# A 32-byte tile first on the left side of SBUF

## The chip, the cores and the metric

The kernel runs on one core of a Trainium2 chip. The metric is the device time of one execution in microseconds (us). The engines are PE (TensorE, matrix products), PEld (its weight loads), DVE (VectorE), ACT (ScalarE), POOL (GpSimd) and SP (SyncE, which issues the DMAs).

## The reference

Two transformer blocks of two layers each run one after the other on a stream of 512 tokens x 1024 channels, all in float32. The first block's layer is

```
h = rms_norm(x, g_mix[l])
q_a, k_a, v_a, u_b, cq, ckv, kpe, gate_logits = split(h @ w_in[l])
y_a, y_b, y_c = swa_attention(...), conformer_conv(...), mla_attention(...)
branches = einsum('bsnc,ncd->bsnd', stack([y_a, y_b, y_c], axis=2), w_branch[l])
x = x + einsum('bsnd,bsnd->bsd', sigmoid(gate_logits), branches) @ w_out[l]
h = rms_norm(x, g_mlp[l])
x = x + square(relu(h @ w_up[l])) @ w_down[l]
```

The second block adds a context of 256 tokens and scales and shifts each norm by a condition (six vectors from `silu(c) @ mod_w + mod_b`). Its first layer mixes with a differential attention and an rwkv7 recurrence, its second with a state space scan and a gated linear attention. Both end as above: `x = x + g1 * (o @ w_out)`, then `x = x + g2 * (square(relu(h @ w1)) @ w2)`, hidden width 4096. Most of the arithmetic is in products of a weight matrix with all tokens.

## The kernel before

Everything is feature-major: a stream is eight tiles of 128 channels x 512 tokens (256 for the context). A weight matrix is read in tiles of 128 rows x up to 1024 values, eight blocks of 128 x 128.

A float32 product is made of three faster ones. `split` (line 196) writes an operand as `hi` + `lo`, both of type fp32r, and `load_w` (line 209) does that to a weight tile: a DMA brings `raw`, ACT casts it to `whi`, DVE writes the rest as `wlo`. `mm3` (line 225) then adds three products into one PSUM tile:

```
t.matmul(ps, w[0], x[0], start=start, stop=False)    # line 228: whi, hi
t.matmul(ps, w[0], x[1], start=False, stop=False)    # line 229: whi, lo
t.matmul(ps, w[1], x[0], start=False, stop=stop)     # line 230: wlo, hi
```

The first operand is the stationary one, the weights (128 x 128); the second is the moving one (128 x 512 or 128 x 256). Each of the three loads its weights anew. `gemm` (line 232) does this for the eight (or four) blocks of an output tile; a group of 24 products of 512 columns in a row is the common case. `gemm_group` and `gemm_level` do it for several output tiles at once.

The order of the work is that of the code: generators are advanced alternately by `weave` (line 176), and each engine takes its instructions as they were written. Waits between engines are added by the framework.

**Where tiles lie.** SBUF is filled from both ends. A pool opened with `side="right"` takes its place downward from the far end, the others upward from the near one, and tiles get addresses rounded to 32 bytes. The first pool on the left is `const` (line 52), with `ident` first; after 16 KiB of scratch and four constants, `ident` stands at byte 16512 of each partition. The streams `x` (`streams`, line 129) and most pools of weights are on the right. The split operands (tags h, hc, u2 and others) are mostly on the left, in the first layer of the second block's mixers and in the last layer's features also on the right. Tiles of a kind all have sizes that are multiples of 512 bytes, so each kind has one place modulo 512.

The table counts the program's fp32r products by the columns of the moving operand and by the start addresses of moving operand and weights modulo 512; d is weights minus moving, modulo 128. The letter is used later.

| group | columns | moving | weights | d | products | where (an example in us) |
|---|---|---|---|---|---|---|
| A (main) | 512 | 192 | 480 | 32 | 7,548 | first block, last MLP (3655 to 3990) |
| B | 512 | 384 | 480 | 96 | 1,536 | `mlp2` of the first layer (3177) |
| C | 256 | 384 | 480 | 96 | 1,744 | the same, context (2665) |
| D | 512 / 256 | 480 | 480 | 0 | 808 / 728 | mixers' inputs, `odd_late` (3400) |
| E | 512 | 416 | 480 | 64 | 416 | mixers' inputs of the first layer |
| F | 256 | 192 | 480 | 32 | 384 | start of the last MLP (3632) |
| G | 512 / 256 | 288 | 288 | 0 | 136 / 168 | `out_proj` (256 columns: 2596) |
| H | 512 / 256 | 288 | 480 | 64 | 120 / 120 | `out_proj`, later tiles (2602 to 2646) |
| I | 512 | 224 | 224 | 0 | 96 | `out_proj`, first tiles (2587) |

Besides, some 4,100 products are in full float32 (small ones in the attentions and recurrences); each is run as two passes, transposes as one.

Of the kernel before, what the change touches and what calls it, by code (L numbers as in the profile page):

```python
# [20 lines left out]
P = 128  # L21
# [6 lines left out]
class Build:  # L28
# [6 lines left out]
    # ---------------------------------------------------------------- helpers  # L35
# [14 lines left out]
    def setup(self):  # L50
        nc = self.nc
        self.const = self.pool("const")
        self.wp = self.xp = None
        self.sp = None
        self.cvs, self.md = {}, []
        self.ident = self.const.tile([P, P], F32, name="ident")
        self.ones = self.const.tile([P, P], F32, name="ones")
        nc.vector.memset(self.ones, 1.0)
        self.mhalf = self.const.tile([P, 32], F32, name="mhalf")
        nc.gpsimd.memset(self.mhalf, -0.5)  # L60

    def consts(self, which, later=False):
        """load a block of packed constants into the innermost phase; later: returns a function that loads it."""
        t = self.tl([P, CV_COLS[which]], F32, "cv")
        self.cvs[which] = t
        load = lambda: self.nc.sync.dma_start(out=t, in_=self.A[which])
        return load if later else load()
# [17 lines left out]
    def phase(self, side=None, **bufs):  # L85
        """chunks with these tags (tag=buffers) while the returned context is open."""
# [18 lines left out]
    def scope(self, attr, **kw):  # L105
        """self.<attr> is a fresh pool while the returned context is open."""
# [17 lines left out]
    def weights(self, parts=2, **kw):  # L124
        """a pool for the weights; parts: tiles of each split part"""
        self.wparts = parts
        return self.scope("wp", **kw)

    def streams(self):
        """a pool for the residual streams, at the far end of the memory"""  # L130
# [26 lines left out]
    def banks(self, **bufs):  # L157
        """PSUM tags (tag=buffers) while the returned context is open."""
# [17 lines left out]
    def weave(main, back=(), until=None):  # L176
        """Alternates the steps of generators: main is [(gen, steps)], kept level until all of them (or the one
        named) end; back is [(task, rate)], tasks that advance rate steps with every main step and may go on later."""
# [16 lines left out]
    # x*scale(+bias) split exactly into two fp32r parts  # L195
# [29 lines left out]
    def mm3(self, ps, w, x, start, stop):  # L225
        """ps (+)= w.T @ x for operands split as (hi, lo)."""
# [5 lines left out]
    def gemm(self, src, xs, n=T, m=P, w=None, tag="g"):  # L232
        """one output tile [m, n] of W.T @ x; src is DRAM [128, kc*m]."""
# [8 lines left out]
    def gemm_group(self, srcs, xs, n=T, ws=None, pieces=1):  # L242
        """several output tiles level in the contraction, for operands that arrive one after another (in pieces of
        their columns); returns their PSUM tiles and weights."""
# [12 lines left out]
    def gemm_level(self, ps, ws, xs, n=T, k0=0, kc=None):  # L257
        """those tiles' products of the operands xs from the k0-th of kc on (a generator)"""
# [18 lines left out]
    def follow(self, x, n=T, split=None, scales=(None,)):  # L277
        """For a norm of a stream whose chunks become final one by one: a function to call after each of them,
        the sums of squares (one per scale) and, with a gain, the split chunks."""
# [14 lines left out]
    def sums(self, accs, n=T, pst="m"):  # L294
        """sums over partitions, token-major: PSUM [128, len(accs) * n / 128]"""
# [13 lines left out]
    def rstd(self, acc, dim, eps, n=T, mul=1.0):  # L309
        """1/sqrt(sum over partitions of acc / dim + eps) * mul, broadcast over partitions."""  # L310
# [3 lines left out]
    def rsqrt_mean(self, acc, dim, eps, n=T):  # L314
        """token-major 1/sqrt(sum over partitions of acc / dim + eps)"""
# [16 lines left out]
    def bcast(self, r, nb, tag="R", pst="m", to=None):  # L332
        """[128 tokens, nb] -> [128, nb*128] with the value of token t in column t of every row."""
# [9 lines left out]
    # ------------------------------------------------------------ first block  # L343
    def prep_rope(self):
        """rope tables for the positions"""
        nc, A = self.nc, self.A
        # --- rope: angles [128 = 4 x (16 | 16), T]; first half of each 32 rows holds -sin
# [37 lines left out]
    def prep_bias(self):  # L385
        """the T5 bias with the band mask, in DRAM"""
        nc, A = self.nc, self.A
        # T5 buckets on the band: column (b, e) of row q is key b*128 + q - 127 + e
# [13 lines left out]
        # rows out of the band: -1e30  # L402
# [18 lines left out]
        # one-hot of the bucket, partition (row group, bucket), against the table in three exact parts  # L421
# [11 lines left out]
        # rows q = 32 j + 8 g + i: g in the one-hot's partitions, j in the output's  # L433
        for i in range(8):
            pb = self.psum("sc")
            for j in range(4):
# [6 lines left out]
                if j % 2:  # L443
                    # the same as 1 - (difference)^2 above zero
# [17 lines left out]
    def gate_in(self, ps, R):  # L462
        """tanh(z/2) of a gemm tile: sigmoid(z) = (1 + tanh(z/2)) / 2."""
# [10 lines left out]
    def layer_first(self, l, x, accs, hs, follow, extra):  # L474
        """follow: for the next norm of x; extra: generators to weave with the MLP."""
# [9 lines left out]
        # ---- MLP  # L485
# [7 lines left out]
    def mix_first(self, l, hs, hacc, prep):  # L493
# [4 lines left out]
        def inputs():  # L498
            # conv branch input: u = a * (1 + tanh(gate/2)); the half goes to the taps
# [23 lines left out]
        # ---- MLA, beside the other branches' inputs  # L523
# [13 lines left out]
        # ---- gates and branches  # L537
# [31 lines left out]
    def mlp(self, hs, acc, up, down, x, after, n=T):  # L569
        """x += relu(h @ up)^2 @ down in four quarters of the hidden width (a generator)"""  # L570
# [21 lines left out]
    def stacks(self, t, keys, tag, n=T):  # L592
        """Splits two heads of 64 rows, for scores in two products: each head's parts in one stack of 128 rows, the
        high one in its own rows, the queries' low one in the other rows, where the keys' high one comes once more;
        and the keys' low parts apart, in their own rows."""
# [11 lines left out]
    def scores(self, ps, q, k, m, qs, ks):  # L607
        """ps = queries (columns qs) times keys (columns ks) of the m-th head of the stacks"""
# [4 lines left out]
    def tok_major(self, src, p=P, nb=4, tag="c"):  # L613
        """[p features, nb*128 tokens] -> [128 tokens, nb, p]"""
# [27 lines left out]
    def conv_ln(self, l, ys, out):  # L642
        """LayerNorm over the channels, swish"""
# [29 lines left out]
    def shuffle16(self, src, p=P):  # L673
        """swap the 16-row halves of every 32 rows."""
# [4 lines left out]
    def mla(self, l, cq, ckv, kpe, out):  # L679
# [4 lines left out]
        # the queries' norm is left to the softmax, as a factor of the scores' rows  # L684
# [6 lines left out]
        # rope of the shared key part  # L691
# [5 lines left out]
        # values, token-major, all heads  # L697
# [61 lines left out]
    def softmax_causal(self, ps, n, scale):  # L759
        """rows of ps[:, :n] (the last 128 columns on the diagonal) times scale -> self.pr, normalised."""  # L760
# [14 lines left out]
    def swa(self, l, q, kk, v, out):  # L775
        nc = self.nc
        sink = self.cvec(f"sink{l}")       # [128, 8]
# [57 lines left out]
    # ----------------------------------------------------------- second block  # L835
    def gemm2(self, src, streams, m=P):
        """one weight tile against several streams [(xs, n)]; returns their PSUM tiles."""
# [4 lines left out]
    def condition(self):  # L842
        """silu of the two conditions [128, 8, 2]; two selectors that sum over partitions into a row each"""
# [14 lines left out]
    def mod(self, i):  # L858
        """the six modulation vectors of both streams: self.md[i] [128, 2 streams, 6, 8]"""
# [6 lines left out]
        for r in range(6):  # L866
            # the second layer's context needs the mixers' shift and scale only
# [34 lines left out]
    def adaln(self, x, n, accs, norm, sc, sh, tag, eps=EPS, pool=None):  # L902
        """rmsnorm(x) * norm * (1 + sc) + sh, split; with a pool: the low parts take x's tiles there. accs: the sums of
        squares, and 1/rms if it is there already."""
# [6 lines left out]
    def early(self, accs, n=T, pst="m", cols=None):  # L911
        """1/rms of a stream (of columns of it), ahead of the tiles it is for"""
# [9 lines left out]
    def adaln_twice(self, x, accs, g, norm, sc, sh, tag, pool):  # L922
        """the same of rmsnorm(x) * g; also returns the inner norm's factors, token-major.
        With m = mean(x^2) + eps both norms' factor is 1/sqrt(mean((x g)^2) + eps m)."""
# [13 lines left out]
    def affine(self, x, n, gs, R, sh, tag, pool=None):  # L938
        """x * gs * R + sh, split, and the function that makes columns of it"""
# [16 lines left out]
    def context(self, md):  # L956
        """the context's input of the second block's first layer (a generator; self.ctx0)"""
# [19 lines left out]
    def layer_even(self, x, accs, px, md, stages):  # L977
        """x comes without the first block's last norm."""
        nc, A = self.nc, self.A
        # the streams wait in DRAM while the mixers run; the low parts of the layer's input take their tiles  # L980
# [4 lines left out]
        with self.phase(feat=14, oa=4, cv=1, **RWC):  # L985
            self.consts("cv3")
            ph = self.phase(side="right", h=8, R=2, tmp=3, raw2=2, ssq=1).__enter__()
            with self.phase(**DAT):
# [4 lines left out]
                with self.banks(g=2, sc=2, tr=1, y=1):  # L993
                    oa = self.diff_attention(first, hl, hc)
                    # beside the last head
# [24 lines left out]
    def out_proj(self, xd, oa, ob, tail, late, md, r1):  # L1020
        """x comes without the first block's last norm (r1); returns the streams, the weights' pool and the streams'
        sums of squares."""
        nc = self.nc
        W = self.A["l0_w_out"]
        with self.phase(h=16), self.banks(g=4, z=2, mm=2):
# [8 lines left out]
            # the last chunks of the mixer go beside the first products  # L1034
# [23 lines left out]
            # the context's last tiles come after the latents', whose norm they hide  # L1058
# [14 lines left out]
    def mlp2(self, i, x, xc, accs, md, pre=None):  # L1073
        """returns the sums of squares of the streams' new values; pre: makes x and the input, in halves"""
        nc, A = self.nc, self.A
        both = xc is not None
        with self.phase(h=16, hc=16, R=2, tmp=3, u2=16, u2c=16), self.banks(g=6, m=1):
# [34 lines left out]
            def down(e, us):  # L1112
                st = [(us[s], streams[s][1]) for s in range(len(streams))]
                ws = []
                # at the end the context comes after the latents, whose norm it hides
# [3 lines left out]
                for c, s in order:  # L1119
                    c2, hf = divmod(c, 2)  # L1120
                    if c2 >= len(ws):
                        # two output tiles share one load: [128, 4 k, 2*128]
# [20 lines left out]
    # ---- differential attention  # L1143
    def diff_inputs(self, h, hl, hc):
        """a head's queries and keys (two maps of 64 rows, turned, as stacks) and its values, token-major"""
# [4 lines left out]
        if h == 0:  # L1150
# [3 lines left out]
            # the context's part first, and the latent's two level: they wait for the latent's norm  # L1154
# [27 lines left out]
    def diff_attention(self, first, hl, hc):  # L1182
        nc, A = self.nc, self.A
        lam_init = 0.8 - 0.6 * math.exp(0.0)
        lv = self.cvec("lam")           # [128, 4]: q1 q2 k1 k2 (rows past 64 are zero)
# [13 lines left out]
        for h in range(4):  # L1199
# [36 lines left out]
            # rmsnorm over the head's 128 features  # L1236
# [7 lines left out]
    # ---- rwkv  # L1244
    def rwkv_features(self, out, hl, hc):
        """the 14 feature chunks after the token shift: r0-3 k0-3 v0-3 (wd|ad) gd, each [128, 256 ctx | 512 lat]
        (a generator: the gates' first, then pair by pair)"""
# [1262 lines left out]
```

## Time and profile before

| | |
|---|---|
| runs, us | 4005.35, 3990.27, 4006.73 (median 4005.35) |
| profiled execution, its span | 4006.0 us (no other time of it is given) |
| PE busy | 3859.9 us, 96% |
| PEld busy | 2984.7 us, 75% |
| DVE busy | 2402.0 us, 60% |
| ACT busy | 1741.8 us, 43% |
| mean granted TensorE clock | 0.967 of 2.4 GHz |

A product's busy time in the trace overlaps that of the next one, since they are pipelined: a product of 512 columns is listed with 0.39 to 0.40 us. What counts is the time from one start to the next, which the timeline gives to 0.01 us, and a count over a stretch more exactly. A stretch in the windows view counts what overlaps it, so on PE one or two products more than start in it; weight loads (PEld) don't overlap each other.

### The profile page before, as it was taken

Reading aid. Unit: us, or ns where it says so; the run is one execution under the profiler, and the core shown is the slowest. Engines: PE = TensorE matmul, PEld = TensorE weight load, DVE = VectorE, ACT = ScalarE, POOL = GpSimd, SP = SyncE. Lnnn points to the kernel's source line nnn. Section 1 sums busy time; section 2 is a strip of 40 time slices with the busy share of each in tenths; the row PEclk is TensorE's granted clock in tenths of the full one; section 3 lists DMA queues with packets and bytes.
Section 4 is the critical chain, followed back from the end, with each engine's and each line's share of the span. In section 5 each row is a group of like instructions: output and inputs, shape, how many; then the busy total and the mean of one; then the engine's idle time right before and its main releaser. Section 6 shows DMA issues by size and latency. Waiting matters only on the chain.

```text
span 4006.0 us, 54862 instructions
## 1 busy us (share of the span) xinstructions
PE 3859.9 (96%) x21506; PEld 2984.7 (75%) x21506; DVE 2402.0 (60%) x4178; ACT 1741.8 (43%) x3923; POOL 80.3 (2%) x171
## 2 busy tenths in 40 slices
PE   8999999999999999999998999999999999889998
PEld 5566877776667777777785666688888887678887
DVE  7587567665785565656646656554444575756444
ACT  4655333334653333334437777532222264533222
POOL 0000000000000000000001000000000000000000
PEclk9999999999999999999998878899999999979999
DMA  3122345441122344431110000211111212012222
GB/s 127 55 88 82 100 147 178 158 136 59 57 92 90 130 164 173 162 114 38 35 52 1 2 2 2 69 53 63 64 63 60 91 48 68 6 61 90 95 95 74
DMA packets 115699, 324.98 MB, mean 81 GB/s; under 512 B 12528, under 2 KB 34032, under 8 KB 115440
## 3 DMA queue, kind: packets, MB, share of 16 engines
q1 hardware_dynamic: 115440, 321.47, 24.4%
q8 instruction: 169, 2.77, 0.3%
q14 instruction: 90, 0.74, 0.1%
HBM read 307.27 MB, written 12.58 MB: 80 GB/s over the span
## 4 chain that ended last, share of the span: by engine, by line
PE 80%; issue 11%; ACT 5%; DVE 3%; POOL 1%; DMA 0%; POOLq 0%; SPq 0%; DVEq 0%; ACTq 0%
PE ps_g L228 20%; PE ps_g L230 20%; PE ps_g L229 20%; PE ps_mm L1562 1%; PE ps_y L748 1%; PE ps_z L1529 1%; PE ps_sc L738 1%; ACT B L1619 1%; POOL r L306 1%; PE ps_sc L611 1%; PE ps_y L823 1%; PE ps_sc L794 1%; PE ps_g L2157 1%; PE ps_y L1234 1%; PE ps_lv L1609 1%
## 5 line engine op out<-in xcount | busy, mean ns | idle before, releaser
L228 PE MATMUL ps_g<-hi,whi 128*128 128x512 f32 (+1 forms) x4464 | 1682.7, 377 | 21.3 <-ACT whi L221 13.7
L230 PE MATMUL ps_g<-hi,wlo 128*128 128x512 f32 (+1 forms) x4464 | 1668.8, 374 | 10.4 <-DVE wlo L222 10.2
L229 PE MATMUL ps_g<-lo,whi 128*128 128x512 f32 (+1 forms) x3744 | 1413.7, 378 | 2.3 <-DVE lo L952 1.8
L221 ACT CAST whi<-raw 128x1024 fp32r<-128x1024 f32 (+3 forms) x497 | 480.7, 968 | 1295.7 <-PE ps_g L229 1120.4
L228 PEld LDWEIGHTS ps_g<-hi,whi 128*128 128x128 f32 x4464 | 845.4, 189 | 205.1 <-ACT whi L221 24.4
L230 PEld LDWEIGHTS ps_g<-hi,wlo 128*128 128x128 f32 x4464 | 845.3, 190 | 183.6 <-DVE wlo L222 18.2
L229 PEld LDWEIGHTS ps_g<-lo,whi 128*128 128x128 f32 x3744 | 707.7, 189 | 148.7 <-issue 10.5
L222 DVE TENSOR_TENSOR wlo<-raw,whi 128x1024 fp32r<-128x1024 f32 (+3 forms) x497 | 557.3, 1122 | 170.4 <-ACT whi L221 165.6
L229 PE MATMUL ps_g<-x,whi 128*128 128x512 f32 (+1 forms) x720 | 253.9, 353 | 0.0
L1128 DVE SCALAR_TENSOR_TENSOR x<-ps_g,mod,x 128x512 f32<-128x512 f32 (+1 forms) x192 | 127.1, 662 | 207.6 <-PE ps_g L230 207.1
L877 DVE SCALAR_TENSOR_TENSOR macc<-mraw,cs,macc 128x1024 f32<-128x1024 f32 x140 | 175.8, 1279 | 4.1 <-DMA mraw<-in_mod_w 3.8
L636 DVE SCALAR_TENSOR_TENSOR cv<-u,taps,cv 128x512 f32<-128x512 f32 x240 | 177.1, 745 | 1.1
L1107 DVE TENSOR_SCALAR r<-ps_g 128x512 f32<-128x512 f32 x96 | 57.6, 602 | 188.5 <-PE ps_g L230 185.6
L229 PEld LDWEIGHTS ps_g<-x,whi 128*128 128x128 f32 x720 | 137.7, 191 | 19.1 <-issue 1.6
L587 DVE TENSOR_TENSOR x<-ps_g,x 128x512 f32<-128x512 f32 x64 | 44.2, 691 | 147.7 <-PE ps_g L230 147.7
L471 DVE TENSOR_TENSOR o<-ps_g,R 128x512 f32<-128x512 f32 x76 | 52.3, 690 | 119.2 <-PE ps_g L230 116.3
L1108 ACT ACTIVATE r<-r 128x512 f32<-128x512 f32 x96 | 53.6, 559 | 146.5 <-DVE r L1107 146.5
L580 DVE SCALAR_TENSOR_TENSOR r<-ps_g,R 128x512 f32<-128x512 f32 x64 | 44.1, 689 | 90.0 <-PE ps_g L230 85.7
L306 POOL TENSOR_TENSOR r<-v,mhalf 128x4 f32<-128x4 f32 (+2 forms) x30 | 39.5, 1316 | 2853.3 <-DVE v L325 2190.3
L202 DVE TENSOR_TENSOR lo<-r,hi 128x512 fp32r<-128x512 f32 x96 | 57.6, 601 | 40.8 <-ACT hi L201 40.8
L1619 ACT COPY B<-ps_lv 32x64 f32<-32x64 f32 x384 | 77.5, 202 | 6.4
L289 ACT ACTIVATE sq<-x 128x512 f32<-128x512 f32 (+1 forms) x91 | 49.1, 542 | 69.5 <-DVE x L1128 34.6
(506 smaller groups left out, 4603.7 us busy)
## 6 DMA issues: line engine op xcount, KB each, us to landing
raw<-in_l_mlp_w SPq DMA_DIRECT2D x128, 512.0 KB, 3.4
mraw<-in_mod_w SPq DMA_DIRECT2D x96, 512.0 KB, 4.5
raw<-in_w_in SPq DMA_DIRECT2D x82, 512.0 KB, 3.5
raw<-in_w_up SPq DMA_DIRECT2D x64, 512.0 KB, 3.5
raw<-in_w_down SPq DMA_DIRECT2D x64, 512.0 KB, 3.5
raw<-in_l_w_in SPq DMA_DIRECT2D x50, 512.0 KB, 3.4
raw<-in_w_branch SPq DMA_DIRECT2D x48, 256.0 KB, 2.7
bias<-biasD SPq DMA_DIRECT2D x16, 512.0 KB, 3.9
```

The source lines that it names most:

```text
L202: nc.vector.tensor_tensor(out=lo, in0=src, in1=hi.bitcast(F32), op=ALU.subtract)
L221: nc.scalar.copy(out=hi, in_=raw)
L222: nc.vector.tensor_tensor(out=lo, in0=raw, in1=hi.bitcast(F32), op=ALU.subtract)
L228: t.matmul(ps, w[0], x[0], start=start, stop=False)
L229: t.matmul(ps, w[0], x[1], start=False, stop=False)
L230: t.matmul(ps, w[1], x[0], start=False, stop=stop)
L306: self.nc.gpsimd.tensor_tensor(out=r, in0=v, in1=self.mhalf[:, :v.shape[1]], op=ALU.pow)
L636: nc.vector.scalar_tensor_tensor(out=y, in0=u[:, j:j + T], scalar=taps[:, c * 31 + j:c * 31 + j + 1], in1=y, op0=ALU.mult, op1=ALU.add)
L877: nc.vector.scalar_tensor_tensor(out=acc[s], in0=rw, scalar=self.cs[:, k, s:s + 1], in1=acc[s], op0=ALU.mult, op1=ALU.add)
L1107: nc.vector.tensor_scalar(out=t, in0=ps[s][:, :n], scalar1=0.0, scalar2=None, op0=ALU.max)
L1128: nc.vector.scalar_tensor_tensor(out=xx[c], in0=ps[:, :n], scalar=md[:, s, 5, c:c + 1], in1=xx[c], op0=ALU.mult, op1=ALU.add)
L1619: nc.scalar.copy(out=B[rows, :, j, :], in_=blocks(ps[rows, 0:64]))
```

## The change

The first pool gets a tile of 8 floats (32 bytes) a partition ahead of `ident`, and POOL sets it to zero. Nothing reads it.

```
     def setup(self):
         nc = self.nc
         self.const = self.pool("const")
+
+        nc.gpsimd.memset(self.const.tile([P, 8], F32, name="shift"), 0.0)
         self.wp = self.xp = None
         self.sp = None
         self.cvs, self.md = {}, []
         self.ident = self.const.tile([P, P], F32, name="ident")
```

The rest of the diff takes comments and descriptions out. `ident` moves from byte 16512 to 16544, and every tile of the left side with it, by 32 bytes; the right side stays where it was. On POOL, at the start of the program (`mhalf` is the third tile of `const`, `u` are inputs of the convolution), before:

```order
L2504 UNCONDITIONAL_BRANCH
L60 MEMSET mhalf 128x32
L509 MEMSET u_614 128x30
L509 MEMSET u_868 128x30
L509 MEMSET u_1159 128x30
L509 MEMSET u_1503 128x30
```

and after (the lines of the file are two further down):

```order
L2506 UNCONDITIONAL_BRANCH
L54 MEMSET shift 128x8
L62 MEMSET mhalf 128x32
L511 MEMSET u_616 128x30
L511 MEMSET u_870 128x30
L511 MEMSET u_1161 128x30
```

The one memset stands ahead of the others. On PE, DVE, ACT and SP the instructions, their order and their waits are the same.

The groups of the table then lie so:

| group | columns | moving | weights | d | products |
|---|---|---|---|---|---|
| A | 512 | 224 | 480 | 0 | 7,548 |
| B | 512 | 416 | 480 | 64 | 1,536 |
| C | 256 | 416 | 480 | 64 | 1,536 (208 stay at 384, 96) |
| D, E | | | | | unchanged |
| F | 256 | 224 | 480 | 0 | 384 |
| G, I | | 320, 256 | 320, 256 | 0 | both operands move, d unchanged |
| H | 512 / 256 | 320 | 480 | 32 | 120 / 120 |

Of the full float32 (and bf16) products 910 get another d, among them those of lines 1529 (368) and 1696 (176) in the rwkv recurrence.

## Rows read from the trace of the kernel before

**Rows 1.** The page: TensorE's share of the span; granted clock in 40 slices, tenths

```profile
PE 3859.9 (96%) x21506; PEld 2984.7 (75%) x21506; DVE 2402.0 (60%) x4178; ACT 1741.8 (43%) x3923; POOL 80.3 (2%) x171
...
PEclk9999999999999999999998878899999999979999
```

**Rows 2.** The page: chain that ended last, by engine, then by line

```profile
PE 80%; issue 11%; ACT 5%; DVE 3%; POOL 1%; DMA 0%; POOLq 0%; SPq 0%; DVEq 0%; ACTq 0%
PE ps_g L228 20%; PE ps_g L230 20%; PE ps_g L229 20%; PE ps_mm L1562 1%; PE ps_y L748 1%; PE ps_z L1529 1%; PE ps_sc L738 1%; ACT B L1619 1%; POOL r L306 1%; PE ps_sc L611 1%; PE ps_y L823 1%; PE ps_sc L794 1%; PE ps_g L2157 1%; PE ps_y L1234 1%; PE ps_lv L1609 1%
```

**Rows 3.** Windows, seventeen stretches of group A; busy us and counts by engine

```profile
core 0: us, PE busy (x) PEld busy (x) DVE busy (x) ACT busy (x) POOL busy (x), PEclk, DMA share, GB/s
357.96:377.33 19.37, 19.37 (x85) 15.59 (x83) 10.59 (x17) 6.69 (x13) 0.00 (x0) 1.00 0.27 81
...
1568.05:1610.97 42.92, 42.92 (x185) 34.57 (x184) 33.77 (x38) 15.92 (x21) 0.00 (x0) 1.00 0.84 294
...
3655.01:3989.59 334.58, 334.58 (x1435) 269.37 (x1434) 164.14 (x189) 100.70 (x127) 0.00 (x0) 1.00 0.27 92
sum 1364.96, PE 1364.96 PEld 1098.89 DVE 793.41 ACT 446.14 POOL 0.29; mean PE 80.29 PEld 64.64 DVE 46.67 ACT 26.24 POOL 0.02
```

**Rows 4.** Timeline, group I, PE: start us, duration us, instruction

```profile
2586.98 0.40 PE L229 MATMUL ps_g<-lo,whi 128*128 128x512 f32 x1
...
2588.36 0.39 PE L229 MATMUL ps_g<-lo,whi 128*128 128x512 f32 x1
2588.58 0.39 PE L230 MATMUL ps_g<-hi,wlo 128*128 128x512 f32 x1
2588.81 0.39 PE L228 MATMUL ps_g<-hi,whi 128*128 128x512 f32 x1
...
2591.98 0.39 PE L230 MATMUL ps_g<-hi,wlo 128*128 128x512 f32 x1
```

**Rows 5.** Timeline, group D with 512 columns, PE

```profile
3400.33 0.39 PE L229 MATMUL ps_g<-x,whi 128*128 128x512 f32 x1
...
3403.05 0.39 PE L229 MATMUL ps_g<-x,whi 128*128 128x512 f32 x1
```

**Rows 6.** Timeline, group H with 512 columns, PE

```profile
2626.55 0.39 PE L228 MATMUL ps_g<-hi,whi 128*128 128x512 f32 x1
...
2637.30 0.39 PE L230 MATMUL ps_g<-hi,wlo 128*128 128x512 f32 x1
```

**Rows 7.** Timeline, group B, PE

```profile
3176.65 0.39 PE L228 MATMUL ps_g<-hi,whi 128*128 128x512 f32 x1
...
3187.66 0.40 PE L230 MATMUL ps_g<-hi,wlo 128*128 128x512 f32 x1
```

**Rows 8.** Timeline, 256 columns, PE: first and last of F, H, G, C

```profile
3632.10 0.28 PE L230 MATMUL ps_g<-hi,wlo 128*128 128x256 f32 x1
...
3652.34 0.28 PE L230 MATMUL ps_g<-hi,wlo 128*128 128x256 f32 x1
...
2607.40 0.28 PE L228 MATMUL ps_g<-hi,whi 128*128 128x256 f32 x1
...
2610.01 0.28 PE L230 MATMUL ps_g<-hi,wlo 128*128 128x256 f32 x1
...
2596.27 0.28 PE L229 MATMUL ps_g<-lo,whi 128*128 128x256 f32 x1
...
2601.79 0.28 PE L230 MATMUL ps_g<-hi,wlo 128*128 128x256 f32 x1
...
2664.57 0.28 PE L228 MATMUL ps_g<-hi,whi 128*128 128x256 f32 x1
...
2670.15 0.28 PE L230 MATMUL ps_g<-hi,wlo 128*128 128x256 f32 x1
```

**Rows 9.** Timeline, group H with 256 columns, a later run, PE

```profile
2643.50 0.28 PE L228 MATMUL ps_g<-hi,whi 128*128 128x256 f32 x1
...
2646.21 0.28 PE L230 MATMUL ps_g<-hi,wlo 128*128 128x256 f32 x1
```

**Rows 10.** Windows, the rwkv recurrence

```profile
2150.00:2550.00 400.00, 373.91 (x4432) 244.89 (x4430) 240.93 (x688) 310.86 (x1262) 17.07 (x25) 0.85 0.01 4
```

**Rows 11.** Timeline, POOL's memset beside which the new one stands

```profile
0.73 0.12 POOL L60 MEMSET mhalf<- 128x32 f32 x1 [0.29 <-POOLq L2500]
```

More of the change, by code (lines that the diff above doesn't have):

```diff
@@ L52, in setup @@
         self.const = self.pool("const")
+        nc.gpsimd.memset(self.const.tile([P, 8], F32, name="shift"), 0.0)
         self.wp = self.xp = None
```

## The prediction

> **What bounds the kernel now.** The page comes first: TensorE is busy for 3859.9 of 4006.0 us, and its granted clock is near the full 2.4 GHz in most slices [rows 1]. A busy share alone does not make a bound, so the chain of waits is next: 80% of the span hangs on PE, and 60 of those points on the three lines of `mm3`, 228 to 230 [rows 2]. Then the view by stretches. Seventeen stretches (the first, the last and one more are shown) hold nothing on PE but 512-column products; PE is busy for every microsecond of their 1364.96 us at clock 1.00, while DVE and ACT have gaps, about half the time in the longest [rows 3]. There the only thing that can move the end is the pace of PE itself: from one start to the next.
>
> That pace isn't what the clock allows. 512 columns at 2.4 GHz would be 213.3 ns. The seventeen stretches (all runs of 64 products or more) hold some 5,850 weight loads, their PEld counts summed, so one product takes 1364.96/5,850 = 233.3 ns. Nothing waits for another engine, so the 20 ns are lost inside TensorE or in what it reads.
>
> The timeline then shows that the pace differs between places that do the same work at the same clock, and the addresses of the program (table in the section on the kernel) sort them. Write d for the weights' address minus the moving operand's, modulo 128. The seventeen stretches have d = 32. Where d = 0:
> - in `out_proj`, after six slower periods (2586.98 to 2588.36, 230 ns each), sixteen periods take 2588.36 to 2591.98, 226.3 ns each [rows 4];
> - in `odd_late`, twelve periods take 2.72 us, 226.7 ns each [rows 5].
>
> At d = 64 (group H), 47 periods take 10.75 us, 228.7 ns each [rows 6]; at d = 96 (group B), 47 take 11.01 us, 234.3 ns [rows 7]. So 512-column products run at 226.7, 228.7, 233.3 and 234.3 ns at d = 0, 64, 32 and 96. The two d = 0 places differ in helper, in the side of the memory and in time, which speaks for the address and against the stage. For 256 columns the order is another: 20.24/171 = 118.4 ns at d = 32, 2.61/23 = 113.5 at d = 64, 5.52/46 = 120.0 at d = 0 and 5.58/47 = 118.7 at d = 96 [rows 8]. Equal distance is the best case for 512 columns and the worst for 256. My reading, not shown: the weight load of the next product runs beside the moving stream, they collide in some cycles, and a run settles into a rhythm in which they collide or don't.
>
> **The change part by part.** No instruction moves on PE, DVE, ACT or SP; POOL gets one memset more. What changes is the address of everything on the left side, by 32 bytes. Weights of the main products are on the right and stay.
>
> 1. *Main products, long stretches.* d goes from 32 to 0. 5,850 x (233.3 - 226.7) = 38.6 us, less a settling start of about 6 x 3.5 ns in each of seventeen stretches, 0.4 us: **-38 us**. Bounds: 0 (no effect) to -39; on the other side the collision case below.
> 2. *Main products, shorter runs.* 7,548 - 5,850 = 1,698 are left. A run that has just begun goes at 230 ns [rows 4], 3.3 less than now; products that stand alone between other work gain nothing. Two thirds of 1,698 x 3.3 ns: **-4 us** (0 to -11, the latter if all settled at once).
> 3. *Groups B and C* (1,536 products of 512 columns and 1,536 of 256, in `mlp2` of the first layer): d goes from 96 to 64. 512 columns: 1,536 x (234.3 - 228.7) = 8.6 us; they alternate with 256-column ones in runs as short as 8, so I take **-7**. 256 columns: 118.7 to 113.5 would be 8.0 us, but another run at d = 64 needs 2.71/23 = 117.8 [rows 9], which would be 1.4; between them **-5**.
> 4. *What gets worse.* Group F (384 of 256 columns) goes to d = 0: 384 x 1.6 ns = 0.6. Group H leaves d = 64 for 32: 120 x 4.6 + 120 x 4.9 ns = 1.1. Together **+2**.
> 5. *Full-precision products.* 910 of them change d, most in the rwkv chain of 2150 to 2550 us, where PE has gaps and the clock is 0.85 [rows 10]. No row there separates distances. If each of two passes lost or won what a 512-column product can (6.6 ns), that were 910 x 2 x 6.6 = 12 us; most have 64 to 256 columns, an eighth to a half, so about 3 us either way. I take **0**.
> 6. *The memset.* The nearest row, four times as wide, takes 0.12 us on POOL at 0.73 us [rows 11]; the first product starts microseconds later, after its first weights and x have come in. **0**. Without that cover it would cost 0.1.
>
> What is late next, when PE hurries? In the longest stretch DVE is busy for 164 and ACT for 101 of 334.6 us and DMA for 0.27 of it; 325 us still hold them. The tightest is the stretch at 1568 us with DMA at 0.84 [rows 3]; were its gain lost, that is 42.92 x 2.8% = 1.2 us, inside the rounding.
>
> Sum: -38 - 4 - 7 - 5 + 2 = -52. The profiled execution spans 4006.0 us and the page gives no time around it; the median of the runs is 4005.35, 0.65 below, so I subtract from the median: 4005.35 - 52 = **3953 us**.
>
> One rule speaks against all of this. The Trainium skill, "TensorE: Matmul & The Clock Gate", section "Step-by-step: what each phase is for", says that TensorE has two separate read ports into SBUF and that loading the next tile's weights takes no read bandwidth from the running product. By that rule terms 1 to 4 are zero. This case's trace disagrees: 226.7 against 233.3 ns at equal clock and equal work. The rule still gets a place among the rivals.
>
> **The rivals.**
> - *Only the distance modulo 512 counts.* The main products will be 256 bytes apart modulo 512, which no product is now; the d = 0 rows all have 0 modulo 512, while d = 64 is 192 in rows 6. For it: nothing in the trace separates 0 from 256. Against: a collision between two streams that both walk on would hardly care for a high bit only. If main products then go at the middling 228.7, term 1 shrinks by 5,850 x 2.0 = 12 us: **3965**.
> - *Addresses don't set the pace; stages do.* The mechanism: the streams don't disturb each other, and the fast places are fast by what else runs there. For it: at d = 0 I have short runs only, none above 40 products. Against: the fast rows come from two stages, and rows 6 and 8 differ by class within 100 us of each other. Then nothing changes: **4005**. (The skill's rule above would give this.)
> - *The main products settle into the colliding rhythm (slower).* At d = 0 the 256-column products settle at 120.0, above the 118.4 of d = 32 [rows 8]. If the 512-column ones at 256 bytes' distance did the same, at two such, 240.0 ns, the place is the seventeen stretches and the price 5,850 x 6.7 = +39 us; with terms 3 and 4, -10, and no term 2, **4034**. It decides once the settled pace is over 233.3 + 10/5.85 = 235 ns. Against it: both d = 0 rows with 512 columns settle low.
>
> **How the numbers follow.** My forecast 0.70; modulo 512 0.14; stages 0.09; colliding rhythm 0.07. The forecast's own range adds the terms' ends: best -39 - 11 - 9 - 8 + 2 - 3 = -68, worst with terms 2 to 4 nearly gone and +3 of term 5 about -33; 3937 to 3972. The range has to take in the second case with the same weak terms, 3972 + 12 = 3984: 3937 to 3984, which leaves the two last rivals out. What a measurement can tell from no change is about 0.5%, 20 us: faster than 3985 in the first two cases and a little of the third, 0.85; within 0.5% most of the third, 0.08; slower the fourth, 0.07.
>
> **What would show it.** In the profile after: the stretch that is 334.58 us long now should take about 1,434 x 226.7 = 325.1 us with the same 1,434 weight loads, all busy; 228.7 a product would point to the second case, 233.3 to the third, 235 or more to the fourth. Runs of 512 columns in `mlp2` of the first layer (now 3176 to 3187 us) should go at about 229 ns, those of 256 columns at 114 to 118. DVE and ACT should hold the same busy time. The forecast is wrong if the long stretches don't shorten, or if they do and the time comes back as new gaps on PE before lines 228 to 230 (waits for `whi` or `wlo`), or if the rwkv stretch grows by more than 3 us.

## The result and the profile after

The changed kernel takes **3960.56 us** (median of 4 runs, 3951.51 to 3964.07) against 4002.18 us (4 runs, 3990.27 to 4006.73): ratio 0.9889, 95% interval [0.9873, 0.9905]. That is -1.1%, 38 to 51 us by the interval. The forecast was 3953, its range 3937 to 3984.

The page after, in the lines that answer to [rows 1, 2] (the lines of `mm3` are 230 to 232 now):

```profile
PE 3807.6 (96%) x21506; PEld 2979.8 (75%) x21506; DVE 2399.7 (61%) x4178; ACT 1741.7 (44%) x3923; POOL 80.0 (2%) x172
...
PEclk9999999999999999999998889899999999879999
...
PE 80%; issue 11%; ACT 5%; DVE 3%; POOL 1%; DMA 0%; POOLq 0%; DVEq 0%; SPq 0%; ACTq 0%
```

PE lost 52.3 us of busy time with the same 21,506 instructions, DVE and ACT kept theirs, and the chain hangs on PE as before. So the time came out of PE itself (7.7 us of it in the rwkv stretch, at the end of this section). The windows of the same seventeen stretches, found by the same PE instructions, answer to [rows 3] (columns as there):

```profile
354.70:373.56 18.86, 18.86 (x85) 15.58 (x84) 10.59 (x17) 6.69 (x13) 0.00 (x0) 1.00 0.28 81
...
1535.63:1577.35 41.72, 41.72 (x186) 34.53 (x184) 33.78 (x38) 15.95 (x21) 0.00 (x0) 1.00 0.86 302
...
3608.01:3933.08 325.07, 325.07 (x1436) 269.14 (x1434) 163.60 (x189) 100.53 (x127) 0.00 (x0) 1.00 0.29 94
sum 1326.32, PE 1326.32 PEld 1097.97 DVE 793.10 ACT 446.68 POOL 0.29; mean PE 78.02 PEld 64.59 DVE 46.65 ACT 26.28 POOL 0.02
```

1364.96 became 1326.32 us, -38.64. The longest went from 334.58 to 325.07, and the stretch at which DMA is busiest (0.84, now 0.86) gave its 1.20 us like the others. PE is busy through all of them: nothing was late next.

The first layer's MLP is the place that did not do what was forecast. One window over 2,976 of its products, before (first line) and after; then, after, the rows that answer to [rows 7] (group B) and [rows 6] (group H):

```profile
2664.57:3187.89 523.32, 523.32 (x2978) 455.00 (x2976) 226.92 (x327) 134.80 (x203) 0.00 (x0) 1.00 0.20 66
```

```profile
2619.47:3141.39 521.92, 521.92 (x2977) 455.15 (x2976) 227.03 (x327) 134.77 (x203) 0.00 (x0) 1.00 0.20 67
3130.20:3141.39 11.19, 11.19 (x50) 9.03 (x49) 6.93 (x10) 3.43 (x6) 0.00 (x0) 1.00 0.40 141
2581.26:2592.23 10.97, 10.97 (x50) 8.82 (x49) 3.49 (x5) 2.04 (x3) 0.00 (x0) 1.00 0.15 49
```

The MLP gained 1.40 us, not 12. Group B needs 11.19/48 = 233.1 ns a product, hardly below the 234.3 of before and far from the 228.7 that d = 64 was to give. Group H, which left d = 64 for 32, needs 10.97/47 = 233.4 ns, as forecast.

The profiled spans differ by 56.5 us (4006.0 and 3949.5), more than the medians; the profiled execution of the changed kernel is the fastest of its four. Part of the difference is the rwkv stretch of [rows 10]. From the same first to the same last of 4,430 periods it took 400.06 us before (first line) and takes 391.93 us after, 8.1 less, at a mean granted clock of 0.88 and not 0.85.

```profile
2150.09:2550.15 400.06, 373.82 (x4431) 244.89 (x4430) 240.89 (x688) 310.92 (x1263) 17.07 (x25) 0.85 0.01 4
2112.79:2504.72 391.93, 366.09 (x4431) 240.32 (x4430) 240.80 (x688) 310.40 (x1263) 17.06 (x25) 0.88 0.01 5
```

Whether these 8 us belong to the change is tested last.

### The profile page after: what moved, and what is told of

It reads as the page before. It is cut to its first block, busy times and chain, and to the rows that moved or that the text cites. A ratio compares the mean times of both kernels' runs of the same rounds, so it can differ in the third digit from the quotient of the medians.

```text
span 3949.5 us, 54863 instructions
## 1 busy us (share of the span) xinstructions
PE 3807.6 (96%) x21506; PEld 2979.8 (75%) x21506; DVE 2399.7 (61%) x4178; ACT 1741.7 (44%) x3923; POOL 80.0 (2%) x172
## 4 chain that ended last, share of the span: by engine, by line
PE 80%; issue 11%; ACT 5%; DVE 3%; POOL 1%; DMA 0%; POOLq 0%; DVEq 0%; SPq 0%; ACTq 0%
PE ps_g L230 20%; PE ps_g L232 20%; PE ps_g L231 20%; PE ps_mm L1564 1%; PE ps_y L750 1%; PE ps_sc L740 1%; PE ps_z L1531 1%; ACT B L1621 1%; POOL r L308 1%; PE ps_g L2159 1%; PE ps_sc L613 1%; PE ps_y L825 1%; PE ps_sc L796 1%; PE ps_y L1236 1%; PE ps_lv L1611 1%
## 5 line engine op out<-in xcount | busy, mean ns | idle before, releaser
L231 PE MATMUL ps_g<-lo,whi 128*128 128x512 f32 (+1 forms) x3744 | 1398.7, 374 | 2.3 <-DVE lo L954 1.8
```

## The experiments

The theories. Theory 1: the distance from the moving operand's address to the weights', modulo 256 (and not 128, as the prediction had it), sets the settled pace of a float32r product. Theory 2: the moving operand's own place modulo 64 does. Theory 3: the stage does, not an address.

**Distances alone.** A program of rows of 48 products on constant tiles; between rows only the distance changes (a and b are byte offsets).

```
def run(n, a, b, k=48):
    for i in range(k):
        nc.tensor.matmul(p[:, :n], wt[:, b // 4:b // 4 + P], mv[:, a // 4:a // 4 + n], ...)
for d in range(16): run(512, 0, 32 * d)
for d in range(16): run(256, 0, 32 * d)
...                 # the other rows, shortened here as the function is
```

> Leaves the whole computation out: it runs rows of 48 products alone, with chosen start addresses of weights and moving operand, nothing beside them. Theory 1 (the distance weights minus moving, modulo 256, sets the settled pace): 512 columns at distances 0, 32, ... 480 go at 226.7, 233, 233, 234, ?, 233, 229, ? ns and then the same eight again; 256 columns at 120, 118, 118, 118, ?, 120, 114, ? and again; both operands 32 bytes further on change nothing. Theory 2 (the moving operand's own place modulo 64 sets it): all sixteen rows of 512 columns are alike at about 233, and the eight rows with both operands 32 bytes on are alike at about 227. Theory 3 (what else runs in a stage sets it): all rows alike. Full float32: 429 ns for 512 columns in two passes at either distance.

The windows over the last 24 periods of each row; first 512 columns at distances 0, 32, 64, ... 224 and 256, then 256 columns at the same nine:

```profile
32.85:38.29 5.44, 5.44 (x26) 4.50 (x25) 0.00 (x0) 0.00 (x0) 0.00 (x0) 1.00 0.00 0
43.88:49.48 5.60, 5.60 (x25) 4.51 (x24) 0.00 (x0) 0.00 (x0) 0.00 (x0) 1.00 0.00 0
55.08:60.68 5.60, 5.60 (x25) 4.51 (x24) 0.00 (x0) 0.00 (x0) 0.00 (x0) 1.00 0.01 3
66.29:71.92 5.63, 5.63 (x26) 4.52 (x24) 0.00 (x0) 0.00 (x0) 0.00 (x0) 1.00 0.00 0
77.49:83.08 5.59, 5.59 (x26) 4.52 (x25) 0.00 (x0) 0.00 (x0) 0.00 (x0) 1.00 0.00 0
88.68:94.28 5.60, 5.60 (x26) 4.50 (x25) 0.00 (x0) 0.00 (x0) 0.00 (x0) 1.00 0.01 3
99.78:105.27 5.49, 5.49 (x25) 4.51 (x24) 0.00 (x0) 0.00 (x0) 0.00 (x0) 1.00 0.00 0
110.87:116.47 5.60, 5.60 (x25) 4.50 (x24) 0.00 (x0) 0.00 (x0) 0.00 (x0) 1.00 0.00 0
121.91:127.35 5.44, 5.44 (x25) 4.50 (x24) 0.00 (x0) 0.00 (x0) 0.00 (x0) 1.00 0.00 0
208.52:211.40 2.88, 2.88 (x27) 2.88 (x25) 0.00 (x0) 0.00 (x0) 0.00 (x0) 1.00 0.00 0
214.24:217.08 2.84, 2.84 (x27) 2.84 (x26) 0.00 (x0) 0.00 (x0) 0.00 (x0) 1.00 0.00 0
219.90:222.73 2.83, 2.83 (x27) 2.83 (x25) 0.00 (x0) 0.00 (x0) 0.00 (x0) 1.00 0.00 0
225.55:228.37 2.82, 2.82 (x27) 2.82 (x26) 0.00 (x0) 0.00 (x0) 0.00 (x0) 1.00 0.00 0
231.20:234.06 2.86, 2.86 (x27) 2.86 (x26) 0.00 (x0) 0.00 (x0) 0.00 (x0) 1.00 0.00 0
236.92:239.80 2.88, 2.88 (x26) 2.88 (x25) 0.00 (x0) 0.00 (x0) 0.00 (x0) 1.00 0.02 6
242.63:245.46 2.83, 2.83 (x27) 2.83 (x26) 0.00 (x0) 0.00 (x0) 0.00 (x0) 1.00 0.00 0
248.28:251.11 2.83, 2.83 (x27) 2.83 (x25) 0.00 (x0) 0.00 (x0) 0.00 (x0) 1.00 0.00 0
253.99:256.87 2.88, 2.88 (x27) 2.88 (x26) 0.00 (x0) 0.00 (x0) 0.00 (x0) 1.00 0.00 0
```

Divided by 24, from the starts in ns:

| distance | 0 | 32 | 64 | 96 | 128 | 160 | 192 | 224 | 256 |
|---|---|---|---|---|---|---|---|---|---|
| 512 columns | 226.67 | 233.33 | 233.33 | 234.46 | 232.67 | 233.33 | 228.88 | 233.33 | 226.67 |
| 256 columns | 120.00 | 118.33 | 117.79 | 117.46 | 118.83 | 120.00 | 117.79 | 117.79 | 120.00 |

Distances of 288 to 480 gave the eight values again within 0.04 ns, both operands 32 bytes on did so too, and 2 to 6 KiB more changed nothing. So in these rows the period is 256, the moving operand's own place doesn't count, and no stage is needed. For 512 columns 64 is a slow distance and 192 the second fastest: the prediction's "d = 64" was read from one group, H at 192, and group B went to 64. Full-precision products of 512 columns took 429 to 430 ns a pass at distances 0 and 32 alike, so 858 ns in their two passes; the expectation had 429 for both.

**The tile on the right, or longer, in the kernel.** Each is the change with one line different:

```
-        nc.gpsimd.memset(self.const.tile([P, 8], F32, name="shift"), 0.0)
+        far = self.ctx.enter_context(self.tc.tile_pool(name="far", bufs=1, side="right"))
+        nc.gpsimd.memset(far.tile([P, 8], F32, name="shift_far"), 0.0)      # on the right side
or
+        nc.gpsimd.memset(self.const.tile([P, 16], F32, name="shift"), 0.0)  # 64 bytes; 40: 160, 64: 256
```

On the right side the weights move and the left side stays: the main distance is 0 modulo 256 with the moving operand still on multiples of 64.

> The left side stays as before; a 32-byte tile stands first on the right side instead, so that the weights lie 32 bytes lower and the main products 256 bytes apart, with moving operands on multiples of 64. Theory 1: main products at 227.2 ns as in the changed kernel, the time within 8 us of it, about 3960. Theory 2: the moving operands haven't moved, so 233.3 ns and about 4002.

> The first tile has 64 bytes instead of 32. Distance of the main products 224, which no kernel so far has; of groups B and C 32. Theory 1 has no value for 224 (between 226.7 and 234; the single rows of products alone give it); B as main before, 233. Theory 2: moving operands on multiples of 64 again, 233.3 ns and about 4002.

> The first tile has 160 bytes. Main products at distance 128, B and C at 448 (192 modulo 256), moving operands 32 off multiples of 64. Theory 1: B at 228.8 and C at 114.4 ns as group H was before, some 10 us less in that stage than the changed kernel; main as the row for 128 says. Theory 2: main at 227 ns, B no better than in the changed kernel, about 3960 in all.

> The tile on the left side has 256 bytes and not 32: every distance between the weights and the moving operand is what it was before modulo 256 (modulo 512 it is not), and every tile lies at another address. Theory 1 (the distance modulo 256 sets the pace): the groups of before again, main products at 233.3 ns, ratio 0.998 to 1.002, about 4003 us. Rival (the distance counts modulo 512 or more, or it is any move of the tiles that helps): under 3985 us.

Measured: right side 3961.73 us, ratio 0.9897 [0.9881, 0.9914]; 64 bytes 3999.42 and 160 bytes 3995.0 us (one run each, before 4003.0); 256 bytes 4001.42 us, ratio 1.0001 [0.9989, 1.0013]. The longest stretch by windows (1,433 periods), of the right side, 64, 160 and 256 bytes:

```profile
3608.66:3933.51 324.85, 324.85 (x1434) 269.04 (x1433) 163.33 (x188) 100.34 (x126) 0.00 (x0) 1.00 0.29 94
```

```profile
3646.55:3980.91 334.36, 334.36 (x1434) 268.56 (x1433) 163.78 (x188) 100.40 (x126) 0.00 (x0) 1.00 0.28 92
```

```profile
3642.30:3976.66 334.36, 334.36 (x1434) 268.95 (x1433) 163.78 (x189) 100.38 (x126) 0.00 (x0) 1.00 0.28 92
```

```profile
3654.89:3989.24 334.35, 334.35 (x1434) 269.18 (x1433) 163.96 (x188) 100.70 (x126) 0.00 (x0) 1.00 0.26 92
```

Main distance 0 gives 226.7 ns from either side; 224, 128 and 32 give 233.3. With 160 bytes the moving operand lies 32 off a multiple of 64, as in the changed kernel, and gains nothing there: theory 2 falls. By the prediction's modulo 128 that kernel (128 apart) would have been as fast as the changed one. With 256 bytes every tile moves, no distance changes modulo 256, and the MLP window takes 523.32 us, the same as before to 0.01 us: a move by itself does nothing. Theory 3 falls by the rows alone, beside which nothing runs, and by the six kernels together: their longest stretch holds the same products beside the same work, and its 1,433 periods are fast at main distance 0 alone. It is the distance.

One expectation came by half: with 160 bytes groups B and C lie at 192, and the MLP was to take some 10 us less than in the changed kernel. It took 4.7 less (517.22 us, in the table below): B went at 229.6 ns, but C at 117.8.

**The MLP's distance alone.** The changed kernel with a gap ahead of the tiles of the first layer's MLP, so that only groups B and C change (208 products of C apart). The changed kernel ran beside them.

```
+    def pad(self, tag, n): self.nc.gpsimd.memset(self.tl([P, n], F32, tag), 0.0)
     # in mlp2, both streams only: 32 floats first (B, C to 192); or 16 floats ahead of hl (B, C to 0);
     # or 16 ahead of hl and u2 and 48 ahead of the context's hc and u2c (B to 0, C stays at 64)
```

> The changed kernel once more, as the measure for the three kernels beside it. Every theory: ratio to the kernel before 0.987 to 0.991, about 3960 us; groups B and C (1,536 products each, distance 64 modulo 256) at about 233.0 and 117.6 ns.

> 128 bytes more ahead of the first layer's MLP tiles: groups B and C go from distance 64 to 192 modulo 256, nothing else moves. Theory 1 (the distance modulo 256 sets the pace): B falls from 233.0 to about 229.7 ns as in the 160-byte kernel, 1,536 x -3.4 = -5 us; C stays at 117.8 or falls to 113.3 ns, 0 to -7 us; 3949 to 3955 us. Rival (the MLP's rows of 12 to 24 products are held by something else, and its distance does not count): B and C unchanged, 3960 us.

> 64 bytes more ahead of the first layer's MLP tiles: groups B and C go to distance 0. Theory 1: B falls to about 227.2 ns, 1,536 x -5.8 = -9 us, and C rises to about 119.9 ns, 1,536 x +2.3 = +3.5 us; about 3955 us. Rival (the MLP's distance does not count): B and C unchanged, 3960 us.

> As the one before, with 192 bytes between the 512-column and the 256-column tiles, so that B lies at distance 0 and C stays at 64. Theory 1: B 227.2 ns, -9 us; C at 117.6 ns, or at 113.3 ns if its rows start as in the kernel with the tile on the right side, 0 to -6 us; 3945 to 3951 us. Rival (the MLP's distance does not count): 3960 us.

The same MLP window in each, in this order, and last in the kernel with the tile of 160 bytes:

```profile
2628.74:3144.87 516.13, 516.13 (x2977) 449.03 (x2976) 226.79 (x327) 134.82 (x203) 0.00 (x0) 1.00 0.20 67
```

```profile
2624.71:3134.34 509.63, 509.63 (x2977) 448.08 (x2976) 226.78 (x327) 134.87 (x203) 0.00 (x0) 1.00 0.21 68
```

```profile
2628.72:3146.42 517.70, 517.70 (x2978) 457.47 (x2976) 226.10 (x325) 134.27 (x202) 0.00 (x0) 1.00 0.20 67
```

```profile
2625.17:3137.95 512.78, 512.78 (x2978) 454.42 (x2977) 227.19 (x327) 135.06 (x203) 0.00 (x0) 1.00 0.20 68
```

```profile
2656.31:3173.53 517.22, 517.22 (x2978) 454.67 (x2976) 227.04 (x327) 135.00 (x203) 0.00 (x0) 1.00 0.20 67
```

Mean period of back-to-back products in these windows, each trace's starts joined with the program's addresses (some 1,395 of B and of C each):

| kernel | B: distance, ns | C: distance, ns | window, us | ratio of times |
|---|---|---|---|---|
| before | 96, 234.1 | 96, 117.7 | 523.32 | |
| after, first trace | 64, 233.1 | 64, **117.7** | 521.92 | 0.9889 [0.9873, 0.9905] |
| after, second trace | 64, 232.9 | 64, **113.7** | 516.13 | 0.9871 [0.9853, 0.9889] |
| B, C at 192 | 192, 228.7 | 192, 113.3 | 509.63 | 0.9854 [0.9835, 0.9873] |
| B, C at 0 | 0, 228.5 | 0, 119.5 | 517.70 | 0.9860 [0.9840, 0.9879] |
| B at 0, C at 64 | 0, 226.7 | 64, 117.7 | 512.78 | 0.9860 [0.9842, 0.9878] |
| tile of 160 bytes | 192, 229.6 | 192, 117.8 | 517.22 | |
| tile on the right side | 64, 232.9 | 64, 113.8 | 516.13 | 0.9897 [0.9881, 0.9914] |

Group B follows its own distance, though at 0 it took 228.5 ns in one kernel and 226.7 in the other, which differ in where C lies. Three things are new. The changed kernel, the same program, had group C at 117.7 ns in one execution and at 113.7 in another, which is most of the 5.8 us between the two windows. At 192, too, C went at 117.8 or 113.3 ns, in two kernels. And the intervals of the four ratios from the second trace down to "B at 0, C at 64" overlap: that B and C at 192 beat the changed kernel by 6 us is shown in the window, not in the times (medians 3953.72 and 3957.81 us). They also compare with each other better than with 0.9889, since six of the nine runs of the kernel before beside them had the lower clock told of under the rwkv stretch.

**What picks the rhythm, and which load collides.** Again rows alone: 256 columns at 64 or 192 behind 24 products of 512 at each distance, or behind one product of 128 to 448 columns; and pairs that take turns.

```
...
for t in (64, 192):
    for d in range(8): run(512, 0, 32 * d, 24); run(256, 0, t, 24)
for t in range(8):
    for n in (128, 160, 192, 288, ...): run(512, 0, 0, 8); run(n, 0, 0, 1); run(256, 0, 32 * t, 24)
```

> Rows of float32r products alone; the kernel's work is left out, and only these rows' paces are read. 1: two moving operands and two weights take turns, so that a product's own weights lie at distance 0 and the next product's at 32, 96 or 128 bytes, or the other way round. Theory 1a (the running product is held by the load of the next product's weights): own distance 0 with the next at 128 gives about 232.7 ns and with the next at 32 about 233.3 ns, own 32 to 128 with the next at 0 gives 226.7 ns. Theory 1b (a product and its own weights collide): the two orders the other way round. 2 to 4: 256-column products behind rows of 512 columns and behind one product of another length. Theory A (at distances 64 and 192 the 256-column product has two rhythms, 113.3 and 117.8 ns, and the moment at which the row begins picks one): both paces appear at these distances, depending on the length of the product ahead of the row, whether both operands lie 32 bytes on or not. Theory B (the pace of 256 columns hangs on a further address): one pace for every place of the operands, whatever runs ahead of the row.

Windows over the last 12 periods of six rows: 256 columns at 64 behind 512 columns at 0, and at 64; 256 columns at 64 behind one product of 160 columns, and of 192; 512 columns at 192, in two rows that began differently.

```profile
237.19:238.60 1.41, 1.41 (x14) 1.41 (x13) 0.00 (x0) 0.00 (x0) 0.00 (x0) 1.00 0.00 0
253.90:255.26 1.36, 1.36 (x14) 1.36 (x13) 0.00 (x0) 0.00 (x0) 0.00 (x0) 1.00 0.04 12
449.59:451.01 1.42, 1.42 (x15) 1.42 (x14) 0.00 (x0) 0.00 (x0) 0.00 (x0) 1.00 0.00 0
454.33:455.69 1.36, 1.36 (x15) 1.36 (x13) 0.00 (x0) 0.00 (x0) 0.00 (x0) 1.00 0.00 0
148.80:151.60 2.80, 2.80 (x13) 2.27 (x12) 0.00 (x0) 0.00 (x0) 0.00 (x0) 1.00 0.00 0
283.00:285.75 2.75, 2.75 (x14) 2.25 (x12) 0.00 (x0) 0.00 (x0) 0.00 (x0) 1.00 0.00 0
```

At 64, 256 columns settle at 117.8 or at 113.3 ns, and the length of the one product ahead is enough to pick: at 64 theory A holds. The 512-column product at 192 has two paces too, 233.3 and 228.9. At distance 0 every row of 512 columns settled at 226.67. At 192, 256 columns went at 117.8 behind every lead, against theory A; that they can go at 113.3 only the kernels showed.

The pairs that take turns fit neither 1a nor 1b: own distance 0 with the next weights at 32, 96, 128 gave 231.67, 233.96 and 228.33 ns; the other way round gave 230.00 all three times. So one product was made odd in a settled row instead.

> Rows of float32r products of 512 columns alone; the kernel's work is left out, and only the starts of the products are read. Each row has 24 products at distance 0, which settle at 226.67 ns, then one with its weights, or its moving operand, or both 32 to 256 bytes on, then 12 at distance 0. Theory 1a (the running product is held by the load of the next product's weights): with the weights moved, the product ahead of the odd one is the first that is longer, by some 2 to 8 ns; with both moved, too. Theory 1b (a product collides with its own weights): the odd product itself is the first, and with both moved nothing changes. At 256 bytes nothing changes by either.

Periods in ns around the odd product, from the starts in the trace (the third is the product ahead of the odd one, the fourth the odd one):

```
weights +32      227 226 235 229 232 231 227 226     operand +32     226 227 227 235 233 233 236 224
weights +128     226 227 233 234 226 227 227 226     operand +128    227 226 227 234 226 227 226 227
weights +160     226 227 237 232 231 227 226 227     operand +160    227 227 226 234 236 233 231 226
weights +192     227 227 226 235 229 232 231 227     operand +192    226 227 227 233 226 236 228 232
weights +256     227 226 227 227 226 227 227 226     operand +256    227 227 226 227 227 226 227 227
```

With the weights moved by 32, 128, 160 or 224, the product *ahead* is the first that gets longer, by 6 to 10 ns (at 96 by 1); with the moving operand moved, never that one but the odd one itself, at all seven distances. With both moved alike (own distance 0), the product ahead again got longer, by 5 to 10 ns at 32, 128, 160 and 224 and by 2 at 96. In these rows each load of the next weights starts 2 to 4 ns after the product ahead and takes 187 to 192 ns, so it lies inside that product. At 32, 96, 128, 160 and 224 this is what theory 1a expects: the running product meets the load of the next product's weights. At 64 and 192 it is not: the product ahead kept its 226 ns and the odd one paid, with the weights moved and with both, which neither theory gives. So what decides is more than one pair, and how the two meet is not shown; this stays open, as do the pairs that take turns. 256 bytes change nothing at all.

**The rwkv stretch.** The kernel before, once more.

> The kernel before once more, for its trace. The rwkv window (4,430 product starts) took 400.06 us in the first trace of it and 402.13 us with the 256-byte tile, and 391.9 to 396.6 us in the seven kernels with other distances. Theory X (the 910 full-precision products that change their distance are faster at the new one): 399 to 403 us again, with the clock's half-speed spells at the same places. Theory Y (the clock's grants differ from execution to execution, whatever the kernel): anything from 391 to 403 us, with the spells elsewhere. The MLP window should take 523.3 us again if the 256-column rhythm at distance 96 is always the same, and less or more if it depends on the execution.

```profile
2149.51:2544.47 394.96, 366.67 (x4431) 239.67 (x4430) 241.18 (x688) 311.10 (x1263) 17.06 (x25) 0.88 0.01 5
2659.62:3183.02 523.40, 523.40 (x2977) 455.11 (x2976) 225.90 (x324) 134.06 (x201) 0.00 (x0) 1.00 0.19 66
```

Without any change the window now takes 394.96 us, at clock 0.88, against 400.06 at 0.85: the grants differ between executions (theory Y). With the 256-byte tile it was 402.13 us at 0.84, in the seven kernels with other distances 391.9 to 396.6 us at 0.87 or 0.88, so the time goes with the clock and not with the distances. Of the 8.1 us at least 5.1 are not the change's, and the other 3 lie within what separates those seven. On one chip nine runs of the kernel before fell in two groups: three at a mean clock of 0.969 took 4000.84 to 4002.99 us, six at 0.964 or 0.965 took 4013.23 to 4016.33. The MLP window is 523.40 us, as it was in the other two traces with groups B and C at 96.

## Why the prediction was right, and where it was not

- *What bounds the kernel: right.* Only the pace of PE moved, and no wait took its place.
- *Term 1, -38: right.* -38.64 us measured, 325.07 us in the longest stretch for 325.1 forecast. The class was too wide, though: "modulo 128" would have promised the same of a main distance of 128, where that stretch took 334.36 us. (The fast products of [rows 4] are group G's by their addresses, not I's; their distance is 0 as well.)
- *Term 2, -4: right.* All back-to-back products of group A went from 233.27 to 227.23 ns, 7,000 x 6.04 = 42.3 us, so 3.6 outside the long stretches.
- *Term 3, -12: the step that failed.* "Write d ... modulo 128" put group H (192) and the new place of group B (64) in one class. The period is 256. B gave 1,536 x 1.0 = 1.5 us for 7. For C the reading of two samples, 113.5 and 117.8 ns at "d = 64" (both at 192), was two rhythms of one distance: 0 us in the first trace, 1,536 x 4.0 = 6 us in the second, for 5 forecast. A warning stood in the trace of before: the table's group E, 416 products of 512 columns at 64 modulo 128 and modulo 256, was not read. They stand two by two with one product of group D (distance 0) between, and such a row took 8.44/36 = 234.4 ns a product at clock 1.00 (line below), not 228.7 or less. A mixed row doesn't give the pace of 64 alone, but it would have opened the bounds of term 3 on the side of nothing.

```profile
1777.95:1786.39 8.44, 8.44 (x37) 6.76 (x36) 4.52 (x16) 1.42 (x3) 0.00 (x0) 1.00 0.00 0
```

- *Term 4, +2: right, in part by luck.* H 120 x 4.6 + 120 x 5.5 = 1.2 us, F 384 x 1.6 = 0.6. H went from 192 to 160, not to 32; for 512 columns the two happen to have one pace (233.33 ns), for 256 they have not (120.0 and 118.3).
- *Terms 5 and 6, 0: not contradicted.* Full precision doesn't separate 0 from 32, and the rwkv window moves as much without the change.
- *The sum.* -38.6 - 3.6 - 1.4 + 1.8 = -41.8 us, or -47.6 with C's faster rhythm, for -52; the medians differ by 41.6, and both sums lie in the interval of 38 to 51. So the gain was missed by 10.4 us and the time by only 7.6, as the forecast was counted from a median of three runs, 4005.35, that a fourth brought to 4002.18. The profiled spans differ by more (56.5), as the rwkv stretch was 8 us shorter at its higher clock, and PE was 38.7 us ahead by the end of group A's first part (1760 us), where the terms give about 33; five other traces with the main distance at 0 were 32.3 to 36.5 ahead there, so this is the execution's, too.
- *The rivals.* "Modulo 512" is refuted: 256 is as good as 0, in the rows alone and in 7,548 products of the kernel. "Stages" is refuted by the rows alone and by the longest stretch, which had two paces beside the same work. "Colliding rhythm" for the main products did not come: distance 0 has one settled pace. But the idea, that a row can lock into a slower rhythm at the same distance, is what group C does.
- *The rule.* By the Trainium skill, "TensorE: Matmul & The Clock Gate", section "Step-by-step: what each phase is for", loading the next weights takes no SBUF read bandwidth from the running product. These traces disagree: the pace hangs on the distance between the two operands, and at five of seven distances the product that ran while moved weights were loaded took 1 to 10 ns longer than its 227.

## What to carry to other kernels

Where rows of products bind and a period is longer than the best row at the same clock, sort the rows by the weights' address minus the moving operand's: for 512 float32r columns a distance of 0 modulo 256 gave 226.7 ns for 233.3, and one small tile ahead of a side sets it. Don't take a period from classes with one sample each; a program of nothing but the rows (620 us here) gives every distance its sample, though a second rhythm may show in the kernel alone, as at 192. Give stages with different distances each their own gap, and read their gain from windows over the same instructions, since medians don't part 5 us here.

## What the runs showed of the hardware beside that

- Several settled paces lie 6.67 ns apart: 226.67 and 233.33 for 512 columns, 113.33 and 120.00 for 256; others lie between. One odd product in a settled row cost 7 to 60 ns in all, spread over up to twelve products, before the periods were back at 226 to 227.
- For 256 columns distances 0 and 160 are the slow end (119.6 to 120.1 in all ten rows behind different leads at each), while for 512 distance 0 is the fast one; 384 columns took 173.33 ns at 0 and 192, 175.75 at 128 and 176.67 at 224; 128 columns 111.67 at the four distances tried.
- Distances below 32 bytes count too: 4, 8 and 16 bytes gave 232.33, 230.50 and 233.33 ns for 512 columns.
